# A hybrid decoder layer on one core: tile starts in SBUF moved to one distance modulo 512 bytes, low parts multiplied after high parts

## The chip, the cores and the metric

The kernel runs on one core of a Trainium2 chip. The time is device microseconds of one execution. The kernel before was timed in three runs, and a fourth execution was profiled; from that one come the rows shown below. The changed kernel is timed in the same way.

The engines are named as in the profile: PE is TensorE's matmul, PEld its load of the stationary operand (the weights of one matmul, 128 columns), DVE is VectorE, ACT ScalarE, POOL GpSimd, and SP issues DMAs.

## The reference: what is computed

One decoder layer on 512 positions of width 2048, in float32, cut to what matters here:

```python
h = rms_norm(x, norm1_w)
q, k, v, z, xbc, dt_raw = jnp.split(h @ w_in, SPLIT_POINTS, axis=-1)
attn = moba_attention(...)      # 8 heads of 128
ssm = ...                       # 16 heads of 64: conv(4), chunked scan, gate, grouped norm
x = x + jnp.concatenate([attn, ssm], axis=-1) @ w_out
h = rms_norm(x, norm2_w)
u = causal_dwconv(h @ w_up, ffn_conv_w, ffn_conv_b)
u_gate, u_val = jnp.split(u, 2, axis=-1)
return x + (jax.nn.silu(u_gate) * u_val) @ w_down
```

The four large products, with `w_in`, `w_out`, `w_up` and `w_down`, are nearly all of the work.

## The kernel before, in words

**Float32 by three products.** A float32 operand is held as a high part (rounded to the format that TensorE reads in one pass, written by ACT) and a low part (the operand minus its high part, written by DVE). A product of two operands is high by high, high by low, and low by high: three matmuls into the same PSUM accumulator. The activations' high and low parts are the tiles `A[k]` and `B[k]` (16 each, 128 x 512); those of a weight piece are the tiles `hi` and `lo`.

**The first stage** (`w_in`, attention, scan, `w_out`) takes its weights through a list of pieces. A chunk of 128 x 1024 is fetched into `raw`, and `issue_split` cuts it in two pieces, each with its own `hi` and `lo` tile from rings of three. The code keeps three pieces ahead: piece i + 3 is split after piece i has been multiplied. Three functions multiply a piece:

- `fm_uses`: features by positions. One accumulator of 512 columns; a piece holds four blocks of 128 x 128. Stationary is `hi` or `lo`, moving is `A` or `B`, 512 columns. A weight column block has four such pieces.
- `wide_use`: the same roles, but a piece is one k with four accumulators.
- `tok_use`: positions by features. Stationary is `A` or `B`, moving is `hi` or `lo`, with 256, 264 or 512 columns, four accumulators.

Between pieces the side work (norms, attention, scan) issues its own short matmuls into the `sm` tiles. The order of all engines is fixed when the program is built; a model of costs in the code (`Paced`) sets where side work is put in.

**The second stage** (`w_up`, `w_down`) multiplies 2 x 2 blocks with seven products in place of eight. A group has seven products, in the order P5, P3 of the group before, P1, P4 of the group before, P6, P2, P7. There are 44 groups for `w_up` (eight blocks of k, so 24 matmuls a product) and 24 for `w_down` (eight or seven blocks, so 24 or 21 matmuls). Stationary is a weight part (`hi2`, `lo2`, two or three buffers of 4096 bytes a partition), moving is one of seven combined activation tiles `cmb0` to `cmb6`, 256 columns. In each product the high parts come first (two matmuls for each block, lines 1288 and 1289) and the low parts last (line 1291). P3 reads `cmb5` (the name `K22` in the code), P4 reads `cmb6`; the other five products read `cmb0` to `cmb4`.

**Where tiles begin.** All numbers here are byte addresses in a partition as the program's allocation gives them, taken modulo 512. "Distance" below is the start of a matmul's moving operand minus the start of its stationary operand, modulo 512. Blocks of 128 columns are 512 bytes, so within a piece the distance stays the same, but for the second half of a piece with 264 columns, which is 32 bytes on.

| matmuls | distance before |
|---|---|
| first stage, `hi` with `A` or `B`, 512 columns moving | 256, 320, 384, by the buffer of the ring |
| first stage, `lo` with `A`, 512 columns moving | 64, 128, 192 |
| first stage, `hi` or `lo` moving | 128 to 480, by the buffer |
| second stage, six products of a group | 448 |
| second stage, P3 (`cmb5`) | 0 |

In the first stage the rings are 528 columns wide (2112 bytes, 64 more than a multiple of 512), so each buffer begins elsewhere. In the second stage a tile `space` of 112 columns (448 bytes) is allocated just before `cmb6`, so `cmb5` begins where the weight tiles begin and `cmb6` 448 bytes on.

## Time and profile before

| | us |
|---|---|
| median of three runs (2103.24 to 2107.04) | 2103.71 |
| profiled execution, its own time | 2103.83 |
| its span from the first to the last instruction | 2102.1 |

The page gives busy time by engine, then the chain of work that ended last, then groups of instructions. Two things are needed to read the rows of PE. A MATMUL's duration in the trace holds its latency, and matmuls overlap: a row's mean of 400 ns does not mean one matmul each 400 ns. What a matmul costs is the distance from its start to the next start, which the timeline shows, and which a window's length over its count of matmuls gives. And a window counts each instruction that reaches into it, so its count is up to two too high.

The stages stand at these times of the span: first stage up to 789 us, the change-over to about 831, `w_up` up to 1640, `w_down` up to the end.

### The profile page before, as it was taken

The page shows a single profiled execution, that of the slowest core. Times are in us where ns is not written, and L with a number is a line of the kernel's source. Part 1 is how long each engine was busy: PE and PEld are TensorE (multiplying, and loading weights), DVE is VectorE, ACT ScalarE, POOL GpSimd, SP SyncE. Part 2 cuts the span into 40 slices and gives each one's busy share as a digit, 9 for nine tenths or more (in the row PEclk, how much of TensorE's full clock was granted, in tenths as well). Part 3 has the DMA queues.
Part 4 walks back from the last instruction along what each step waited for, and adds up shares of the span by engine and source line. Part 5 has one row for each costly group of instructions (what it writes and reads, how often), then busy time and mean ns, then how long its engine had stood idle before and what let it go on. Part 6 is the DMA issues. An engine that isn't in the chain of part 4 may idle for free.

```text
span 2102.1 us, 37694 instructions
## 1 busy us (share of the span) xinstructions
PE 2061.9 (98%) x15366; PEld 1938.7 (92%) x15366; DVE 1582.6 (75%) x2251; ACT 988.3 (47%) x1433; POOL 207.9 (10%) x107
## 2 busy tenths in 40 slices
PE   9999999999999998999999999999999899999999
PEld 7888887888888888999999999999999799899999
DVE  6545555345565548999999999999999977977976
ACT  5433435244444435555555554555555534534532
POOL 0020000000000001101110111111111111101110
PEclk9999999999999999999999999999999999999999
DMA  5232222332224445445444444444355667856753
GB/s 196 73 116 91 71 72 79 92 109 81 79 72 162 158 134 193 158 152 191 151 154 178 167 162 159 165 181 161 141 191 202 216 214 245 272 188 232 261 202 121
DMA packets 114397, 328.19 MB, mean 156 GB/s; under 512 B 10736, under 2 KB 35120, under 8 KB 111408
## 3 DMA queue, kind: packets, MB, share of 16 engines
q1 hardware_dynamic: 114224, 325.78, 45.0%
q8 instruction: 121, 1.98, 0.4%
q14 instruction: 52, 0.43, 0.1%
HBM read 283.77 MB, written 41.98 MB: 155 GB/s over the span
## 4 chain that ended last, share of the span: by engine, by line
PE 90%; DVE 6%; DMA 2%; issue 1%; ACT 1%; SPq 0%; DVEq 0%; POOL 0%; ACTq 0%; POOLq 0%
PE acc L183 30%; PE x L1288 16%; PE x L1289 16%; PE x L1291 16%; PE sm L183 4%; PE y L1288 3%; PE y L1289 3%; PE y L1291 3%; DVE lo L1050 1%; DVE cmb L1097 1%; DMA rawa<-wd 1%; DMA ld<-gd 0%; DVE lo L183 0%; DVE acc L1153 0%; DVE s L1024 0%
## 5 line engine op out<-in xcount | busy, mean ns | idle before, releaser
L1289 PE MATMUL x<-cmb,hi 128*128 128x256 f32 x3168 | 748.5, 278 | 13.2 <-DVE cmb L1097 11.5
L1288 PE MATMUL x<-cmb,hi 128*128 128x256 f32 x3168 | 749.1, 278 | 11.9 <-ACT cP L1168 5.4
L1289 PEld LDWEIGHTS x<-cmb,hi 128*128 128x128 f32 x3168 | 597.4, 189 | 16.1 <-DVE cmb L1097 14.3
L1288 PEld LDWEIGHTS x<-cmb,hi 128*128 128x128 f32 x3168 | 596.9, 188 | 14.4 <-issue 7.9
L1291 PE MATMUL x<-cmb,lo 128*128 128x256 f32 x3168 | 430.3, 278 | 2.2 <-DVE lo L1050 2.0
L1291 PEld LDWEIGHTS x<-cmb,lo 128*128 128x128 f32 x3168 | 393.4, 189 | 2.7 <-DVE lo L1050 2.7
L183 DVE TENSOR_TENSOR lo<-raw,hi 128x512 fp32r<-128x512 f32 (+1 forms) x240 | 164.4, 691 | 242.3 <-ACT hi L183 227.7
L1041 ACT ACTIVATE hi<-s 128x1024 fp32r<-128x1024 f32 (+1 forms) x201 | 200.8, 999 | 284.8 <-DVE s L1024 190.4
L1017 POOL TENSOR_TENSOR rawb<-rawa,rawb 128x1024 f32<-128x1024 f32 (+1 forms) x68 | 169.6, 2495 | 1298.3 <-DVE s L1024 1061.8
L183 PE MATMUL acc<-A,hi 128*128 128x512 f32 x704 | 281.5, 400 | 0.7 <-ACT hi L183 0.7
L183 PE MATMUL acc<-A,lo 128*128 128x512 f32 x704 | 277.9, 395 | 0.1
L183 PE MATMUL acc<-B,hi 128*128 128x512 f32 x704 | 276.9, 393 | 0.0
L183 ACT ACTIVATE hi<-raw 128x512 fp32r<-128x512 f32 (+1 forms) x240 | 149.6, 629 | 255.7 <-PE acc L183 222.5
L1050 DVE TENSOR_TENSOR lo<-s,hi 128x1024 fp32r<-128x1024 f32 (+1 forms) x201 | 238.4, 1186 | 18.8 <-issue 18.8
L1050 DVE TENSOR_TENSOR lo<-rawa,hi 128x1024 fp32r<-128x1024 f32 (+1 forms) x204 | 241.5, 1184 | 3.9 <-PE x L1291 3.9
L1041 ACT ACTIVATE hi<-rawa 128x1024 fp32r<-128x1024 f32 (+1 forms) x204 | 209.6, 1028 | 40.2 <-PE x L1289 40.0
L183 PEld LDWEIGHTS acc<-A,lo 128*128 128x128 f32 x704 | 132.2, 188 | 32.3 <-DVE lo L183 1.4
L183 PEld LDWEIGHTS acc<-A,hi 128*128 128x128 f32 x704 | 132.8, 189 | 29.0 <-ACT hi L183 1.3
L183 PEld LDWEIGHTS acc<-B,hi 128*128 128x128 f32 x704 | 132.5, 188 | 28.3
L1168 ACT ACTIVATE cP<-x 128x256 f32<-128x256 f32 x132 | 50.8, 384 | 211.2 <-PE x L1291 211.2
L183 PE MATMUL acc<-hi,A 128*128 128x256 f32 (+2 forms) x448 | 135.5, 302 | 0.7 <-DVE u L183 0.7
L183 PE MATMUL acc<-lo,A 128*128 128x256 f32 (+2 forms) x448 | 133.7, 298 | 0.0
(204 smaller groups left out, 2775.1 us busy)
## 6 DMA issues: line engine op xcount, KB each, us to landing
rawa<-wu SPq DMA_DIRECT2D x176, 512.0 KB, 3.3
raw<-wi SPq DMA_DIRECT2D x79, 512.0 KB, 3.6
rawa<-wd SPq DMA_DIRECT2D x64, 448.0 KB, 4.2
rawb<-wu SPq DMA_DIRECT2D x44, 512.0 KB, 4.3
gd<-gt SPq DMA_DIRECT2D x22, 1024.0 KB, 4.4
raw<-wo SPq DMA_DIRECT2D x32, 512.0 KB, 3.5
rawa<-wd SPq DMA_DIRECT2D x32, 512.0 KB, 4.4
ld<-gd SPq DMA_DIRECT2D x27, 512.0 KB, 6.3
```

Of the source, the lines that this page charges most:

```text
L183: return fn(out, *args, **kw)
L1017: po.tensor_tensor(r, raw[gi, "11"][:, :n], r, op=OP.subtract)
L1041: se.activation(h[:, :n], src[:, :n], AF.Copy)
L1050: ve.tensor_tensor(l[:, :n], src[:, :n], h[:, :n].bitcast(F32), op=OP.subtract)
L1097: ve.tensor_tensor(lo, ld[:, :m, :], hi.bitcast(F32), op=OP.subtract)
L1168: se.activation(g[x], X[:, 256:] if x == "P5" else X[:, :256], AF.Copy)
L1288: pe.matmul(out, w, bk[:, 0, q, :], start=fresh and q == 0, stop=False, skip_group_check=True)
L1289: pe.matmul(out, w, bk[:, 1, q, :], start=False, stop=False, skip_group_check=True)
L1291: pe.matmul(out, l[:, q * 128:(q + 1) * 128], bk[:, 0, q, :], start=False, stop=q == n - 1, skip_group_check=True)
```

## The change

**Distances.** The rings `hi` and `lo` become 640 columns wide (2560 bytes, a multiple of 512), a tile `space` of 448 bytes is put before `A`, and pieces for `tok_use` begin 96 columns (384 bytes) into their tiles. The `space` of the second stage is allocated before `cmb5` in place of before `cmb6`. With that, by the allocation, every large product of both stages is at distance 448 (the second half of a 264-column piece at 480), but for some low parts.

**Low parts at distance 0.** Some pieces' low parts begin 112 columns (448 bytes) into their tile, which puts them at distance 0: the last of the four pieces of a column block in `fm_uses`; k = 3, 7, 11 in `wide_use`; the pieces with k0 = 4 and 8 in `tok_use`; and P3 of every fourth group of `w_up` and of every group of `w_down`. These are 176 matmuls with 512 columns, 64 with 256 and 32 with 264 in the first stage, and 264 in the second.

**Order.** In all pieces of `fm_uses`, and in those pieces of `wide_use` and `tok_use` whose low parts are at distance 0, all products with high parts are issued first and those with low parts last. No matmul, no transfer and no operation of ACT, DVE or POOL is added or taken away.

| matmuls | distance after |
|---|---|
| `A` with `hi`, `B` with `hi`, 512 columns | 448 (1408) |
| `A` with `lo`, 512 columns | 448 (536), 0 (168) |
| `hi` or `lo` moving, 512 columns | 448 (184), 0 (8) |
| moving, 256 columns, first stage | 448 (704), 0 (64) |
| moving, 264 columns | 448 and 480 (352), 0 and 32 (32) |
| second stage | 448 (10824), 0 (264) |

On PE, one piece of `fm_uses` in the first stage, before (`A_81` to `A_84` and `B_97` to `B_100` are the parts of four activation tiles):

```order
L183 MATMUL acc<-A_81,hi 128x512
L183 MATMUL acc<-B_97,hi 128x512
L183 MATMUL acc<-A_81,lo 128x512 [waits DVE_49]
L183 MATMUL acc<-A_82,hi 128x512
L183 MATMUL acc<-B_98,hi 128x512
L183 MATMUL acc<-A_82,lo 128x512
L183 MATMUL acc<-A_83,hi 128x512
```

The same piece now (the tiles' numbers are one higher):

```order
L183 MATMUL acc<-A_82,hi 128x512
L183 MATMUL acc<-B_98,hi 128x512
L183 MATMUL acc<-A_83,hi 128x512
L183 MATMUL acc<-B_99,hi 128x512
L183 MATMUL acc<-A_84,hi 128x512
L183 MATMUL acc<-B_100,hi 128x512
L183 MATMUL acc<-A_85,hi 128x512
L183 MATMUL acc<-B_101,hi 128x512
L183 MATMUL acc<-A_82,lo 128x512 [waits DVE_49]
L183 MATMUL acc<-A_83,lo 128x512
L183 MATMUL acc<-A_84,lo 128x512
L183 MATMUL acc<-A_85,lo 128x512
```

The four low parts, and the wait for DVE that stands before the first of them, have moved from between the high parts to the end of the piece.

DVE keeps its order, and so do ACT, POOL and SP; some of DVE's waits are others. At the change-over, before (`acc_s` is the first sum of the second stage):

```order
L183 TENSOR_TENSOR lo<-raw,hi 128x512 [waits PE_49,Activation_49]
L183 TENSOR_TENSOR rbc<-rbc,sq 128x512 [waits DVE_49,Activation_49]
L1024 TENSOR_TENSOR acc_s<-rawb,rawa 128x1024 [waits DMAHW4_49,DMAHW3_49]
L1050 TENSOR_TENSOR lo_7088<-acc_s,hi_7086 128x1024 [waits PE_49,Activation_49]
L183 TENSOR_TENSOR xin<-acc,xin 128x512 [waits DMAHW0_49,PE_49]
```

And now:

```order
L183 TENSOR_TENSOR lo<-raw,hi 128x512 [waits PE_49,Activation_49]
L183 TENSOR_TENSOR rbc<-rbc,sq 128x512 [waits DVE_49,Activation_49]
L1055 TENSOR_TENSOR acc_s<-rawb,rawa 128x1024 [waits DMAHW3_49,DMAHW4_49,DVE_49,PE_49]
L1083 TENSOR_TENSOR lo_7089<-acc_s,hi_7087 128x1024 [waits Activation_49]
L183 TENSOR_TENSOR xin<-acc,xin 128x512 [waits DMAHW0_49,PE_49]
```

`acc_s` now lies over one of the `lo` tiles of the last but one piece, and waits until PE has read it.

The diff:

```diff
@@ -210,6 +210,10 @@
 
 
     RW = 1024
+    WT, SHIFT_T, SHIFT_0 = 640, 96, 112
     BEHIND = 2.5
     pieces = []
 
@@ -245,12 +249,13 @@
             i = state["split"]
             ci, o, w, _ = pieces[i]
             issue_dma(ci)
-            h = wpool.tile([128, 528], F32R, name="hi")
-            l = wpool.tile([128, 528], F32R, name="lo")
+            ho, lo = getattr(pieces[i][3], "at", (0, 0))
+            h = wpool.tile([128, WT], F32R, name="hi")[:, ho:ho + w]
+            l = wpool.tile([128, WT], F32R, name="lo")[:, lo:lo + w]
             src = raws[ci][:, o:o + w]
             clk["last"] = ("pe", clk["pe"])
-            A_.activation(h[:, :w], src, AF.Copy)
-            V.tensor_tensor(l[:, :w], src, h[:, :w].bitcast(F32), op=OP.subtract)
+            A_.activation(h, src, AF.Copy)
+            V.tensor_tensor(l, src, h.bitcast(F32), op=OP.subtract)
             his[i] = (h, l)
             ready[i] = clk["dve"]
             state["split"] += 1
@@ -260,6 +265,7 @@
             nc.sync.dma_start(dbg[n], ap)
 
 
+    abp.tile([128, 112], F32, name="space")
     A = [abp.tile([128, S], F32R, name=f"A{k}") for k in range(NK)]
     B = [abp.tile([128, S], F32R, name=f"B{k}") for k in range(NK)]
     C = [cpool.tile([128, S], F32, name=f"C{k}") for k in range(NK)]
@@ -643,13 +649,19 @@
             def use(h, l, k0=k0, nk=nk):
                 if k0 == 0:
                     box["acc"] = acc_tile()
+                a = box["acc"]
+                w = lambda x, kk: x[:, kk * 128:(kk + 1) * 128]
                 for kk in range(nk):
                     k = k0 + kk
                     rh, rl = R(k)
-                    mm3(box["acc"], h[:, kk * 128:(kk + 1) * 128], l[:, kk * 128:(kk + 1) * 128], rh, rl,
-                        k == 0, k == nk_tot - 1)
+                    T.matmul(a, w(h, kk), rh, start=k == 0, stop=False)
+                    T.matmul(a, w(h, kk), rl, start=False, stop=False)
+                for kk in range(nk):
+                    T.matmul(a, w(l, kk), R(k0 + kk)[0], start=False, stop=k0 + kk == nk_tot - 1)
                 if k0 + nk == nk_tot:
-                    done(box["acc"])
+                    done(a)
+            if k0 + nk == nk_tot:
+                use.at = (0, SHIFT_0)
             uses.append(use)
             k0 += nk
         return uses
@@ -662,11 +674,21 @@
             if k == 0:
                 box["acc"] = [acc_tile() for _ in range(4)]
             rh, rl = R(k)
+            if k % 4 == 3 and k < NK - 1:
+                for t in range(4):
+                    ts_ = slice(t * 128, (t + 1) * 128)
+                    T.matmul(box["acc"][t], h[:, ts_], rh, start=False, stop=False)
+                    T.matmul(box["acc"][t], h[:, ts_], rl, start=False, stop=False)
+                for t in range(4):
+                    T.matmul(box["acc"][t], l[:, t * 128:(t + 1) * 128], rh, start=False, stop=False)
+                return
             for t in range(4):
                 ts_ = slice(t * 128, (t + 1) * 128)
                 mm3(box["acc"][t], h[:, ts_], l[:, ts_], rh, rl, k == 0, k == NK - 1)
                 if k == NK - 1:
                     done(t, box["acc"][t])
+        if k % 4 == 3 and k < NK - 1:
+            use.at = (0, SHIFT_0)
         return use
 
     def tok_use(k0, nk, cols, box, done):
@@ -675,6 +697,13 @@
             if k0 == 0:
                 box["acc"] = [acc_tile() for _ in range(4)]
             edge = k0 == 0 or k0 + nk == NK
+            if again:
+                for part, x in ((h, A), (h, B), (l, A)):
+                    for kk in range(nk):
+                        for t in range(4):
+                            T.matmul(box["acc"][t][:, :cols], x[k0 + kk][:, t * 128:(t + 1) * 128],
+                                     part[:, kk * cols:(kk + 1) * cols], start=False, stop=False)
+                return
             order = [(kk, t) for t in range(4) for kk in range(nk)] if edge else \
                     [(kk, t) for kk in range(nk) for t in range(4)]
             for kk, t in order:
@@ -687,6 +716,8 @@
                 T.matmul(o, B[k][:, ts_], h[:, cc], start=False, stop=k == NK - 1)
                 if k == NK - 1:
                     done(t, box["acc"][t])
+        again = k0 in (4, 8)
+        use.at = (SHIFT_T, SHIFT_0 if again else SHIFT_T)
         return use
 
     XR = lambda k: (A[k], B[k])
@@ -1046,7 +1077,9 @@
             return
         n = cols(items[k][0])
         h, src = parts[k]
-        l = lp.tile([128, 1024], F32R, name="lo2", bufs=2)
+        l = lp.tile([128, 1152], F32R, name="lo2", bufs=2)
+        if items[k][1] == "P3" and (items[k][0] % 4 == 0 or items[k][0] >= NF and items[k][0] % 1 == 0):
+            l = l[:, SHIFT_0:]
         ve.tensor_tensor(l[:, :n], src[:, :n], h[:, :n].bitcast(F32), op=OP.subtract)
         parts[k] = (h, l)
 
@@ -1125,7 +1158,7 @@
 
     def x_split(n):
         t, h = (K22, KT4)[n // 2], n % 2
-        if n == 2:
+        if n == 0:
             lp.tile([128, 112], F32, name="space")
         if h == 0:
             up_kinds[t] = cmb_tile(t)
```

## The prediction

> **What bounds the kernel now.** I read the page's first lines and its chain, then busy time by stage, then PE alone in order of time. The first two rows are the page's, the other four those of a view by windows (window, length, busy us of each engine, granted clock, share and rate of DMA):
>
> ```profile
> PE 2061.9 (98%) x15366; PEld 1938.7 (92%) x15366; DVE 1582.6 (75%) x2251; ACT 988.3 (47%) x1433; POOL 207.9 (10%) x107
> PE 90%; DVE 6%; DMA 2%; issue 1%; ACT 1%; SPq 0%; DVEq 0%; POOL 0%; ACTq 0%; POOLq 0%
> ...
> 0.00:789.30 789.30, 781.78 (x4266) 664.86 (x4266) 414.32 (x794) 340.27 (x639) 36.32 (x38) 1.00 0.33 106
> 789.30:831.00 41.70, 33.62 (x269) 33.05 (x270) 32.47 (x41) 20.16 (x29) 6.68 (x3) 0.92 0.57 202
> 831.00:1640.00 809.00, 809.00 (x7082) 809.00 (x7081) 761.05 (x947) 426.62 (x550) 104.09 (x43) 1.00 0.46 166
> 1640.00:2102.00 462.00, 437.53 (x3755) 431.75 (x3753) 374.79 (x472) 201.24 (x216) 60.77 (x24) 1.00 0.64 221
> ```
>
> PE bounds every stage but the 40 us of change-over: it idles 7.5 us in the first stage, nothing in `w_up`, 24.5 us in `w_down`. No other engine is near it in the first stage (DVE 414 of 789 us); in `w_up` DVE has 48 us to spare in 809. So what a matmul costs, start to start, is the question. PE in order of time, three products of one `w_up` group (P3, P1, P4; start, duration, with the first high part of each, the row of its eight low parts, and the start of the next product):
>
> ```profile
> 834.58 0.28 PE L1288 MATMUL x<-cmb,hi 128*128 128x256 f32 x1
> ...
> 837.30 0.28 PE L1288 MATMUL x<-cmb,hi 128*128 128x256 f32 x1
> ...
> 839.20 1.12 PE L1291 MATMUL x<-cmb,lo 128*128 128x256 f32 x8
> 840.16 0.29 PE L1288 MATMUL x<-cmb,hi 128*128 128x256 f32 x1
> ...
> 842.90 0.28 PE L1288 MATMUL x<-cmb,hi 128*128 128x256 f32 x1
> ...
> 844.72 1.07 PE L1291 MATMUL x<-cmb,lo 128*128 128x256 f32 x8
> 845.62 0.28 PE L1288 MATMUL x<-cmb,hi 128*128 128x256 f32 x1
> ```
>
> P5 (834.58 to 837.30) and P4 (842.90 to 845.62) take 2.72 us for 24 matmuls, 113.3 ns each. P3, the one product at distance 0, takes 2.86 us: 118.8 ns for a high part, 120.0 for a low part, and the product behind it 2.74. Same shapes, same engine, nothing waited for: what differs is where `cmb5` begins. I read this as the weight load and the moving stream meeting in SBUF.
>
> Distance 448 alone does not give 113.3, though. At the change-over, `cmb` products at distance 448, then the first P3 of the program (818.08):
>
> ```profile
> 811.99 0.28 PE L1288 MATMUL x<-cmb,hi 128*128 128x256 f32 x1
> ...
> 813.87 1.10 PE L1291 MATMUL x<-cmb,lo 128*128 128x256 f32 x8
> ...
> 818.08 0.28 PE L1288 MATMUL x<-cmb,hi 128*128 128x256 f32 x1
> ...
> 819.99 1.12 PE L1291 MATMUL x<-cmb,lo 128*128 128x256 f32 x8
> ...
> 822.79 1.08 PE L1291 MATMUL x<-cmb,lo 128*128 128x256 f32 x8
> ...
> 825.51 1.07 PE L1291 MATMUL x<-cmb,lo 128*128 128x256 f32 x8
> ```
>
> Sixteen high parts in 813.87 − 811.99 = 1.88 us are 117.5 ns each: a slower rhythm that began behind a stall and held, at 448, until P3's run at distance 0; from the low parts of the product behind P3 to those of the next, 822.79 to 825.51, it is 113.3 again (2.72 / 24). So 448 has two rhythms, and a run at distance 0 ends the slow one. That is what I take the low parts at distance 0 to do in the changed kernel.
>
> The first stage has neither. Windows over accumulator matmuls alone (264, 512, 256 columns moving, then 512 columns of `A` and `B`), and the counts:
>
> ```profile
> 95.98:125.28 29.30, 29.30 (x241) 1.00 0.38 109
> 381.40:425.60 44.20, 44.20 (x193) 1.00 0.29 92
> 473.60:490.60 17.00, 16.99 (x144) 1.00 0.22 64
> 640.00:770.00 130.00, 128.73 (x556) 1.00 0.51 166
> ...
> L183 PE MATMUL acc<-A,hi 128*128 128x512 f32 x704 | 281.5, 400 | 0.7 <-ACT hi L183 0.7
> L183 PE MATMUL acc<-hi,A 128*128 128x256 f32 x256 | 73.5, 287 | 0.0
> L183 PE MATMUL acc<-hi,A 128*128 128x264 f32 x128 | 36.8, 288 | 0.7 <-DVE u L183 0.7
> L183 PE MATMUL acc<-lo,A 128*128 128x512 f32 x64 | 25.2, 394 | 0.0
> ```
>
> With 512 columns a matmul costs 231.5 ns (128.73 / 556; 230 where `A` is stationary, 44.20 / 192), with 256 columns 118.1 (17.00 / 144), with 264 columns 122.1 (29.30 / 240); the pieces stand at all three distances of the rings. Each row of counts stands three times (high-high, high-low, low-high): 3 × (704 + 64) = 2304 with 512 columns, 768 with 256, 384 with 264. The first is 533 us, two thirds of the stage.
>
> **The change part by part.** The sum is made against the profiled execution's 2103.83 us; the median of the runs is 0.12 lower.
>
> *P3.* In 33 groups of `w_up` all of P3 goes to 448: 2.86 + 2.74 becomes 2 × 2.72, 0.16 us each, 5.3. In 11 groups and the 24 of `w_down` only its high parts do: 16 × (118.8 − 113.3) = 0.09 us, 35 × 0.09 = 3.1. Together 8.4. If it were hidden by DVE it would be nothing; DVE's 761 of 809 us leaves 1.1 us a group, seven times the gain. `w_down` has waits in which part of its 2.1 may vanish.
>
> *The 512-column matmuls.* No row shows one in a stream at 448, so its cost is bounded. From above: 231.5, no gain. From below, the half clock at the change-over, where 256 columns take as long as 512 at full clock (ten starts on):
>
> ```profile
> 801.05 0.41 PE L1289 MATMUL x<-cmb,hi 128*128 128x256 f32 x1
> ...
> 803.18 0.42 PE L1289 MATMUL x<-cmb,hi 128*128 128x256 f32 x1
> ```
>
> 2.13 us / 10 = 213 ns, so 256 columns at full clock are 106.5 and the fast rhythm adds 6.8 to that. The same 6.8 on 213 gives 220; the slow rhythm (11 more than 106.5) 224. Pieces here are cut by side work and stalls, after which either rhythm may come, and the runs at distance 0 stand some 11 us apart (48 × 231 ns); two thirds fast, a third slow gives 221.5, and I take 222. That is 9.5 ns on the 2304 − 176 = 2128 matmuls at 448: 20.2 us. The ends are 0 and 18.5 × 2128 = 39 us.
>
> The Trainium skill ("TensorE: Matmul & The Clock Gate", Back-to-back issue gap) states N / 2.4 + 2.5 ns, 215.8 for 512 columns; by that the term would be an estimated 33 us. For 256 columns it gives 109.2, which no stretch of this trace reaches (113.3).
>
> *256 and 264 columns.* 118.1 to about 114.5 on 704, 2.5 us; 122.1 to 118 on 352, 1.4 us (ends 0 and 3.4 + 1.9).
>
> *Order and waits.* The same matmuls and loads run in another order. PE waited for DVE's low parts before and does so eight matmuls later now, which can only shorten a wait; such waits are 7.5 us of the stage at most. DVE's new waits stand where a `lo` ring buffer is read last in its piece; the next write is three pieces ahead, and behind it stand only side vector operations. I cost them at nothing; uncovered, the low parts of a piece (8 × 0.12 us) on 14 pieces would be 13 us of DVE, which is idle for 375 us there. At the change-over `acc_s` waits for the last but one piece:
>
> ```profile
> 785.32 0.40 PE L183 MATMUL acc<-A,lo 128*128 128x512 f32 x1
> 785.56 0.40 PE L183 MATMUL acc<-A,hi 128*128 128x512 f32 x1
> ...
> 785.95 1.22 DVE L1024 TENSOR_TENSOR acc_s<-rawb,rawa 128x1024 f32<-128x1024 f32 x1 [3.44 <-DMA rawa<-wu]
> ```
>
> That piece ends at 785.56, `acc_s` starts at 785.95 on a DMA: 0.4 us of cover. Without it the whole change-over shifts by as much. Transfers follow the same rings, so they start earlier with PE, at a third of the DMA engines' time.
>
> Sum: 8.4 + 20.2 + 2.5 + 1.4 = 32.5 us. 2103.83 − 32.5 = 2071.3, less 0.12: **2071**.
>
> **The rivals.**
>
> *Only the 256-column matmuls feel the distance.* With 512 columns the load takes half of the stream, and may find its way anywhere. For it: no row shows it otherwise; against it: 231.5 is 18 above 213, more than the 256's 11.6, so something costs there, and a matmul in three at 448 among others at other distances could not settle. 2103.7 − 8.4 − 2.5 − 1.4 = 2091.
>
> *The loss at 512 vanishes whole.* 214 to 217 ns: 14.5 to 17.5 × 2128 = 31 to 37 us, with the other terms 2055 to 2061. For it: the weight load has half the stream free. Against it: no stretch at full clock shows less than 6.8 of overhead.
>
> *The slow rhythm holds.* The place is P3 of the first group: before, 24 matmuls at distance 0 ended the slow rhythm, now 8 have to. If 8 are too few, `w_up` runs at 117.5: a group costs 7 × 2.82 = 19.74 us against 6 × 2.72 + 2.88 = 19.20, 44 × 0.54 = 24 us more, and `w_down` up to 13 more. The first stage, with the same short runs, then stays at 224 at best and 231.5 at worst: 2103.7 + 24 − 16 = 2112 to 2127, say 2118. It decides when a run leaves the next product above 117. Against it: in P3 at 837.30 the high parts are at 118.8 on average, near its low parts' 120, so the state turns early.
>
> *The distance is not the cause.* P3 might be slow for its place in the group. The Trainium skill ("SBUF — State Buffer", Who interferes with whom) says that PE never waits on anyone, and that its two read ports are independent; by that rule a distance would cost nothing; the trace differs, with 2.86 against 2.72 us. Were P3's place the cause, the change would move nothing: 2103.7. For its place speaks nothing in the rows: it reads and writes as P6 does.
>
> **How the numbers follow.** My forecast (222 ± 3 ns with 512 columns: 2064 to 2079) 0.57; only 256-column matmuls 0.20; the loss vanishes whole 0.12; slow rhythm 0.06; distance not the cause 0.05. The range takes in the forecast, the first two rivals and their bounds: 2055 to 2094; the forecast's own is 2064 to 2079. A measurement of this kernel tells 0.2% (4 us) from no change. Faster: 0.57 + 0.20 + 0.12 = 0.89; within 0.2%, where the distance is not the cause: 0.05; slower, the slow rhythm: 0.06.
>
> **What would show it.** Right: windows over 512-column pieces in 640 to 750 at 219 to 225 ns a matmul; P3 as long as P4 in three of four `w_up` groups; a product behind a run of low parts at 113 to 114 after a stall; the first stage some 24 us shorter, the change-over as long. Wrong: 231 ns in the first stage; 117.5 ns over many groups of `w_up`; new waits for DVE in PE's rows, above all in `w_up`, where DVE's share rises to 95%.

## The result, and the profile after

The changed kernel takes 2136.08 us (median of four executions, 2134.34 to 2138.36) where the kernel before takes 2104.42 (2103.24 to 2107.04): a ratio of 1.0149, 95% interval 1.0132 to 1.0167. It is slower by some 32 us. I had said 2071, faster, with 0.06 for slower.

First the page of the changed kernel (busy time by engine; chain by engine), then its stages by windows (window, length, busy us and count of PE, PEld, DVE, ACT, POOL, granted clock, share and rate of DMA). The ends of the windows are put where the stages end now.

```profile
PE 2100.5 (98%) x15366; PEld 1974.2 (92%) x15366; DVE 1587.3 (74%) x2251; ACT 988.2 (46%) x1433; POOL 208.4 (10%) x107
PE 90%; DVE 7%; issue 2%; ACT 1%; DMA 1%; SPq 0%; DVEq 0%; POOL 0%; ACTq 0%; POOLq 0%
...
0.00:792.00 792.00, 785.53 (x4266) 664.95 (x4266) 415.52 (x795) 339.86 (x639) 36.69 (x38) 1.00 0.33 105
792.00:833.50 41.50, 32.70 (x262) 31.92 (x263) 32.47 (x39) 20.07 (x29) 6.75 (x3) 0.92 0.58 203
833.50:1666.70 833.20, 833.20 (x7098) 833.20 (x7097) 764.94 (x950) 428.18 (x551) 105.64 (x43) 1.00 0.44 162
1666.70:2136.00 469.30, 449.05 (x3745) 444.15 (x3744) 374.37 (x470) 200.10 (x214) 59.32 (x24) 0.99 0.63 216
```

The instruction counts, the chain and DVE's time are those of before. `w_up` takes 833.2 us where it took 809.0 (the window now holds 16 matmuls more, some 2 us; `w_down` lacks ten); `w_down` 469.3 for 462.0; the first stage 792.0 for 789.3; the change-over 41.5 for 41.7. From the first matmul of group 2 to that of group 44, the same work in both, it is 828.8 us (837.88 to 1666.63) for 806.4 (834.58 to 1640.98), and from there to the end 466.9 for 458.1. In `w_up` PE never idles in either kernel, so each matmul costs more there: 117.4 ns (833.20 / 7098) for 114.2.

Where it turns can be seen on one page of PE in order of time (start, duration; the first high part of a product, or its row of eight low parts). These are P5 and then P3 of group 4, the second P3 with low parts at distance 0, then P1, P4 and P6:

```profile
895.00 0.28 PE L1321 MATMUL x<-cmb,hi 128*128 128x256 f32 x1
...
897.72 0.28 PE L1321 MATMUL x<-cmb,hi 128*128 128x256 f32 x1
...
899.53 1.12 PE L1324 MATMUL x<-cmb,lo 128*128 128x256 f32 x8
900.49 0.28 PE L1321 MATMUL x<-cmb,hi 128*128 128x256 f32 x1
...
903.32 0.28 PE L1321 MATMUL x<-cmb,hi 128*128 128x256 f32 x1
...
906.14 0.28 PE L1321 MATMUL x<-cmb,hi 128*128 128x256 f32 x1
```

P5 takes 2.72 us, and the sixteen high parts of P3, now at 448, 1.81 (113.1 ns each): the fast rhythm, with P3 in it, as predicted. The eight low parts at distance 0 take 0.96 (120 ns). Behind them P1 takes 2.83 and P4 2.82 us, 117.7 ns a matmul, and so it stays to the end of `w_up`, over nine more runs at distance 0. What I had put there to end the slow rhythm starts it, and doesn't end it.

The first stage, windows over accumulator matmuls alone (512, 256, 264 columns):

```profile
640.00:770.00 130.00, 128.10 (x550) 1.00 0.50 164
475.70:492.40 16.70, 16.66 (x144) 1.00 0.21 65
96.50:125.60 29.10, 29.09 (x241) 1.00 0.36 104
```

With 512 columns a matmul costs 128.10 / 550 = 232.9 ns, more than the 231.5 of before (from start to start in that window 233.1 for 232.3, as the counts take in two matmuls too many); with 256 columns 116.0 (118.1 before), with 264 columns 121.3 (122.1).

### The profile page after: what moved, and what is told of

It reads as the page before. It is cut to its first block, busy times and chain, and to the rows that moved or that the text cites. A ratio compares the mean times of both kernels' runs of the same rounds, so it can differ in the third digit from the quotient of the medians.

```text
span 2136.7 us, 37701 instructions
## 1 busy us (share of the span) xinstructions
PE 2100.5 (98%) x15366; PEld 1974.2 (92%) x15366; DVE 1587.3 (74%) x2251; ACT 988.2 (46%) x1433; POOL 208.4 (10%) x107
## 4 chain that ended last, share of the span: by engine, by line
PE 90%; DVE 7%; issue 2%; ACT 1%; DMA 1%; SPq 0%; DVEq 0%; POOL 0%; ACTq 0%; POOLq 0%
PE acc L183 30%; PE x L1324 16%; PE x L1322 16%; PE x L1321 16%; PE sm L183 4%; PE y L1322 3%; PE y L1324 3%; PE y L1321 3%; DVE lo L1083 2%; DVE cmb L1130 1%; DVE acc L1186 0%; DVE s L1055 0%; DVE lo L183 0%; DVE s L1061 0%; DMA t<-xT 0%
## 5 line engine op out<-in xcount | busy, mean ns | idle before, releaser
L1321 PE MATMUL x<-cmb,hi 128*128 128x256 f32 x3168 | 766.4, 281 | 11.8 <-ACT cP L1201 7.5
L1322 PE MATMUL x<-cmb,hi 128*128 128x256 f32 x3168 | 766.0, 281 | 10.0 <-DVE cmb L1130 10.0
L1324 PE MATMUL x<-cmb,lo 128*128 128x256 f32 x3168 | 440.0, 281 | 2.6 <-DVE lo L1083 2.6
L1324 PEld LDWEIGHTS x<-cmb,lo 128*128 128x128 f32 x3168 | 401.4, 189 | 3.2 <-DVE lo L1083 3.2
L183 PE MATMUL acc<-A,lo 128*128 128x512 f32 x704 | 205.1, 395 | 0.0
L1322 PE MATMUL y<-cmb,hi 128*128 128x256 f32 x528 | 128.0, 282 | 3.1 <-DVE cmb L1130 3.1
L1321 PE MATMUL y<-cmb,hi 128*128 128x256 f32 x528 | 127.6, 281 | 0.0
```

The source lines that it names most:

```text
L183: return fn(out, *args, **kw)
L1321: pe.matmul(out, w, bk[:, 0, q, :], start=fresh and q == 0, stop=False, skip_group_check=True)
L1322: pe.matmul(out, w, bk[:, 1, q, :], start=False, stop=False, skip_group_check=True)
L1324: pe.matmul(out, l[:, q * 128:(q + 1) * 128], bk[:, 0, q, :], start=False, stop=q == n - 1, skip_group_check=True)
```

## The experiments

In all of them "at 448" and so on is the distance as defined above, "rhythm" is the start-to-start time of 256-column matmuls, 113.3 ns or 117.8 ns, and a shift of 16 columns is 64 bytes. A P3 is named by its own group; it runs behind P5 of the next. Numbers in ns without a row are the same kind of difference between starts as those with one.

### Which stage loses

Second stage of the changed kernel behind the first stage of the kernel before (the diff is against the kernel before):

```diff
+        l = lp.tile([128, 1152], F32R, name="lo2", bufs=2)
+        if items[k][1] == "P3" and (items[k][0] % 4 == 0 or items[k][0] >= NF and items[k][0] % 1 == 0):
+            l = l[:, 112:]
-        if n == 2:
+        if n == 0:
             lp.tile([128, 112], F32, name="space")
```

> The kernel before with the second stage of the changed one alone (space ahead of cmb5, eight low parts at distance 0); the first stage keeps its rings of 528 columns and its order. If the second stage holds the whole loss: 2131 to 2136 us, the first stage as before. If the first stage lost the time: about 2104 us.

And the first stage of the changed kernel with the second stage of the kernel before (against the changed kernel):

```diff
-        l = lp.tile([128, 1152], F32R, name="lo2", bufs=2)
-        if items[k][1] == "P3" and (items[k][0] % 4 == 0 or items[k][0] >= NF and items[k][0] % 1 == 0):
-            l = l[:, SHIFT_0:]
+        l = lp.tile([128, 1024], F32R, name="lo2", bufs=2)
-        if n == 0:
+        if n == 2:
             lp.tile([128, 112], F32, name="space")
```

> The changed kernel with the second stage of the one before (cmb5 and so all of P3 at distance 0, cmb6 at 448). If the first stage neither gained nor lost (512 columns at 448 cost 233.2 ns against 231.5, 256 columns 116.5 against 118): 2103 to 2108 us, the second stage at 113.4 ns outside P3. If the first stage's order or distances hold the loss: about 2134 us.

The second stage alone: 2138.09 us, ratio 1.0156 (1.0139 to 1.0173). The first alone: 2104.98, ratio 0.9998 (0.9989 to 1.0008). One window of `w_up` of each (second stage alone, then first stage alone):

```profile
830.00:1640.00 810.00, 810.00 (x6878) 810.00 (x6878) 741.36 (x921) 413.55 (x533) 100.77 (x41) 1.00 0.44 162
```

```profile
830.00:1640.00 810.00, 810.00 (x7090) 810.00 (x7089) 761.86 (x947) 426.52 (x550) 103.87 (x43) 1.00 0.46 166
```

810 us hold 6878 matmuls (117.8 ns) in the one and 7090 (114.2) in the other. So the whole loss is the second stage's, and the first stage is worth nothing either way (the 2.7 us by which it was longer in the changed kernel's profiled execution don't come back in these ten). In the second stage alone `w_up` came out of the change-over in the slow rhythm, and none of eleven runs at distance 0 ended it.

### The runs at distance 0 taken out

The changed kernel without its shifted low parts in the second stage:

```diff
         l = lp.tile([128, 1152], F32R, name="lo2", bufs=2)
-        if items[k][1] == "P3" and (items[k][0] % 4 == 0 or items[k][0] >= NF and items[k][0] % 1 == 0):
-            l = l[:, SHIFT_0:]
```

> The changed kernel, but in the second stage no low part is put at distance 0: all of it stands at 448. Theory A (a run of eight low parts at distance 0 throws PE from the 113.4 ns rhythm into the 117.8 ns one, and at 448 either rhythm lasts until something disturbs it): w_up stays at 113.4 ns once it is there, some 30 us less in w_up and up to 12 less in w_down, 2094 to 2106 us. Theory B (at 448 PE falls into the slow rhythm by itself and only whole P3 products at 0, 24 matmuls each group, pull it out): 117.8 ns throughout, 2132 to 2142 us.

Its ten executions fall in two groups, so a ratio means nothing: 2094.82 to 2098.53 (four) and 2125.87 to 2130.29 (six), with 2105.08 for the kernel before beside them. The profiled one is of the second group:

```profile
830.00:1640.00 810.00, 810.00 (x6880) 810.00 (x6879) 741.28 (x920) 413.95 (x534) 100.78 (x41) 1.00 0.44 161
```

117.7 ns in all of `w_up`, at 448 throughout. In `w_down` of the same execution, behind waits, there are long stretches at 113.3 with the same starts. So both rhythms keep themselves going at 448, and which one comes behind a stall is not fixed by the starts. That the quick group had `w_up` at 113.3 was not seen in a trace, but the gap fits: 43 groups by 168 matmuls by 4.5 ns are 32.5 us, and the groups lie 27 to 35 us apart.

### Is it the length of the run?

Changed kernel; in `w_up` P3 of some groups has whole, low or high parts shifted by a table (`hi2` is 1152 columns wide, too; nothing is shifted in `w_down`):

```diff
+    W, L, H = (112, 112), (0, 112), (112, 0)
+    RUNS = {1: W, 3: W, 5: L, 7: L, 9: H, 11: H, 13: W, ..., 20: (0, 16), 23: (0, 32), 26: (0, 64), 29: (0, 96), ...}
-        h = lp.tile([128, 1024], F32R, name="hi2", bufs=3)
+        h = lp.tile([128, 1152], F32R, name="hi2", bufs=3)
+        h = h[:, RUNS.get(gi, (0, 0))[0] if x == "P3" else 0:]
```

> The changed kernel with another table of runs at distance 0 in P3 of w_up: by group the whole product (16 high and 8 low parts), its 8 low parts alone, its 16 high parts alone, or none, and in four groups the low parts at 384, 320, 192 or 64; none in w_down. Theory A: behind 8 low parts at 0 the rhythm is 117.8 ns whichever it was ahead, behind a whole product 113.4 ns whichever it was ahead, and groups with none keep the rhythm that they come in with. Theory B: whole products lead to 113.4 ns, groups with none fall back to 117.8. The 16 high parts alone and the low parts at other distances are open: no number is expected.

2126.85 us (one execution). PE in order of time: P3 of group 1, whole at distance 0, then P1 and the start of P4:

```profile
838.72 0.28 PE L1324 MATMUL x<-cmb,hi 128*128 128x256 f32 x1
...
841.60 0.28 PE L1324 MATMUL x<-cmb,hi 128*128 128x256 f32 x1
...
844.42 0.28 PE L1324 MATMUL x<-cmb,hi 128*128 128x256 f32 x1
```

P3 takes 2.88 us (120.0 ns), and P1 behind it 2.82 (117.5). All 24 matmuls at distance 0, as many as in the kernel before, and the slow rhythm holds; so it did behind every run of the table (all were entered slow, so what they leave behind the fast rhythm this execution doesn't show). That the run was merely too short fell with this. The eight low parts alone at 384, 320, 192 or 64 (groups 20, 23, 26, 29) left it slow as well. What is left as a difference: in the kernel before, the moving tile `cmb5` begins elsewhere and the weights stay; here the weights begin elsewhere and `cmb5` stays.

### Runs made by the moving tile

Kernel before, with `cmb5` where it was (32 bytes past a multiple of 512, the other `cmb` 480), and P3's weights shifted by a table:

```diff
+    Z, F = (0, 0), (16, 16)
+    RUNS = {0: Z, 3: (16, 0), 4: (16, 0), 5: Z, 6: (0, 16), 7: (0, 16), 8: Z, 9: (16, 0), 10: Z, 11: Z, 12: (32, 32), ...}
+    run_of = lambda gi: RUNS.get(gi, F)
+        h = h[:, run_of(gi)[0] if x == "P3" else 0:]
+        l = l[:, run_of(items[k][0])[1] if items[k][1] == "P3" else 0:]
```

> The kernel before with one change: in P3 the weight parts begin some columns into their tiles, by a table (hi2 and lo2 are 1152 columns wide). cmb5 stays where it was, 32 bytes past a multiple of 512, so P3 is at distance 0 without a shift, at 448 with a shift of 16 columns, at 384, 320, ... with 32, 48, ... . In the run with the table of shifted weights the runs at distance 0 were made by moving the weights, and none of them, not even a whole P3, ended the slow rhythm; in the kernel before the weights stay and the moving tile begins elsewhere. Theory C (what ends the slow rhythm is a whole run at distance 0 that is entered and left by the moving operand's start): groups 0, 5, 8, 11, 13, ... (whole P3 at 0) leave 113.3 ns behind them, whatever was ahead; groups with 16 columns (448) change nothing; low parts alone at 0 (groups 3, 4, 9) or high parts alone (6, 7) may leave either, and I expect 117.8 behind low parts alone, as in the changed kernel; from group 24 on, all at 448, the rhythm stays what group 23 left, 113.3. Time near 2095 to 2103. Rival (the exit is chance, and the kernel before was lucky in its alignment): whole runs at 0 leave 117.8 in some groups and 113.3 in others; time 2100 to 2126.

2102.5 us (one execution). P3 of group 3 (high parts at 448, the eight low parts alone at 0), with P1 and the start of P4; then P3 of group 15 (whole at 0), which comes out of the slow rhythm:

```profile
875.08 0.28 PE L1296 MATMUL x<-cmb,hi 128*128 128x256 f32 x1
...
876.97 1.12 PE L1299 MATMUL x<-cmb,lo 128*128 128x256 f32 x8
877.93 0.29 PE L1296 MATMUL x<-cmb,hi 128*128 128x256 f32 x1
...
880.66 0.28 PE L1296 MATMUL x<-cmb,hi 128*128 128x256 f32 x1
...
1105.86 0.28 PE L1296 MATMUL x<-cmb,hi 128*128 128x256 f32 x1
...
1108.73 0.29 PE L1296 MATMUL x<-cmb,hi 128*128 128x256 f32 x1
...
1111.47 0.28 PE L1296 MATMUL x<-cmb,hi 128*128 128x256 f32 x1
```

Eight low parts at distance 0 are followed by 2.73 us (877.93 to 880.66), the fast rhythm; against my expectation for low parts alone. The whole run, entered at 117.8, is followed by 2.74. So 24 matmuls at distance 0 end the slow rhythm here and did not in the table before: at the same length, the place of the tiles decides. Eight of them keep the fast rhythm here, where in the changed kernel eight ended it; whether eight would also end the slow one here was not run. In what it says of whole runs at 0 theory C held: behind none of them was the rhythm left slow, and the rival fell. One thing came out that no theory had: the high parts of group 3, at 448, cost 118.1 (1.89 / 16) between products at 113.5 and 114.1. With both tiles 64 bytes on, the same distance is in the other rhythm, and going back restores the first.

| P3's distance (`cmb5` at 32) | P3, ns, entered at 113.3 | P1 behind it |
|---|---|---|
| 0 and 256 | 119.2 | 114.1 (fast) |
| 128 and 384 | 118.3, 118.4 | 114.1 (fast) |
| 192 and 448 | 117.6 | 114.2 (fast) |
| 64 and 320 | 113.4 | 117.9 (slow) |

Distances 256 bytes apart behave alike.

### Whole runs kept, but rare

The kernel before with the same two lines and another rule in place of the table, P3 at 448 by a shift of 16 columns but for every eighth group of `w_up` and every second of `w_down`:

```diff
+    run_of = lambda gi: (0, 0) if gi % (8 if gi < NF else 2) == 0 else (16, 16)
```

> The kernel before, with P3 at distance 448 by weights that begin 16 columns into their tiles, except in every eighth group of w_up and every second of w_down, where P3 stays whole at distance 0 as before. First stage as before. Theory C: the first P3 ends the slow rhythm as in the kernel before, every eighth would again, and the other P3 take 2.72 us in place of 2.86, the product behind them 2.72 for 2.74: 38 groups of w_up by 0.16 and 12 of w_down by 0.16 are 8.0 us, so 2105 - 8 = 2097, in every execution. Rival (rhythm by chance): some executions near 2097, others near 2126, as in the run with no runs at distance 0.

2102.71 us (2101.80 to 2104.80), ratio 0.999 (0.998 to 0.9999). All ten executions are near there, so the fast rhythm holds in each, but the gain is 2.5 us and not 8. P3 of group 11, then P1 and the start of P4:

```profile
1029.62 0.28 PE L1292 MATMUL x<-cmb,hi 128*128 128x256 f32 x1
...
1032.44 0.29 PE L1292 MATMUL x<-cmb,hi 128*128 128x256 f32 x1
...
1035.18 0.28 PE L1292 MATMUL x<-cmb,hi 128*128 128x256 f32 x1
```

P3 takes 2.82 us and P1 2.74, not 2.72 each: 448 with both tiles 64 bytes on is not 448.

### What a 512-column matmul costs at each distance

Changed kernel; each column block of `fm_uses` has its parts 16 columns further than the block before, modulo eight (`sweep` counts the pieces, four to a block); the blocks of `tok_use` with 256 and 264 columns are moved in the same way:

```diff
-            if k0 + nk == nk_tot:
-                use.at = (0, SHIFT_0)
+            use.at = (sweep(),) * 2
```

> The changed kernel with other starts in its first stage: each column block of fm_uses has its high and low parts 16 columns further than the block before it, modulo eight, so blocks stand at distances 448, 384, 320, ... 0; blocks of tok_use with 256 and 264 columns move likewise. What each theory expects of 512 columns: if the distance sets the cost of a 512-column matmul at all, some distance shows clearly under 231 ns in its undisturbed stretches (my prediction's 222 would be one of them), and I would have chosen the wrong one; if 512 columns don't feel it, all eight distances stand within 2 ns of each other at 231 to 233. I expect the second: the kernel before had 230 to 231.7 at nine starts, the changed one 231.2 at 0 and 233.3 at 448. The second stage is that of the changed kernel, so the time is near 2136 in both cases.

In `w_out` such blocks follow each other without a break. These are the starts of nine blocks of 48 matmuls, at distances 384, 320, 256, 192, 128, 64, 0, 448 and 384:

```profile
664.91 0.39 PE L183 MATMUL acc<-A,hi 128*128 128x512 f32 x1
...
676.07 0.40 PE L183 MATMUL acc<-A,hi 128*128 128x512 f32 x1
...
687.07 0.40 PE L183 MATMUL acc<-A,hi 128*128 128x512 f32 x1
...
697.97 0.40 PE L183 MATMUL acc<-A,hi 128*128 128x512 f32 x1
...
709.17 0.39 PE L183 MATMUL acc<-A,hi 128*128 128x512 f32 x1
...
720.33 0.40 PE L183 MATMUL acc<-A,hi 128*128 128x512 f32 x1
...
731.32 0.40 PE L183 MATMUL acc<-A,hi 128*128 128x512 f32 x1
...
742.22 0.40 PE L183 MATMUL acc<-A,hi 128*128 128x512 f32 x1
...
753.42 0.39 PE L183 MATMUL acc<-A,hi 128*128 128x512 f32 x1
```

| distance | us for 48 | ns each |
|---|---|---|
| 0, 256 | 10.90, 10.90 | 227.1 |
| 64, 320 | 10.99, 11.00 | 229.0 |
| 128, 384 | 11.16, 11.16 | 232.5 |
| 192, 448 | 11.20, 11.20 | 233.3 |

This expectation was wrong, on the side of the other theory: 512 columns do feel the distance, modulo 256, and 448 is the dearest of the eight. My forecast went to the right variable and to the wrong end of it. The kernel as a whole took 2135.64 us (one execution); its second stage is that of the changed kernel.

The table is one for blocks that stand at one distance, and here only the weights were moved. The kernel before mixes distances within a piece. By the table its pieces of `w_out` should cost, on the mean of a piece, 227.7 ns (high parts at 256, low parts at 64), 230.2 (320 and 128) and 232.8 (384 and 192); between 655 and 778 us of its trace they cost 232.6, 232.9 and 231.7, with a low part behind every two high parts. With the same starts and the low parts last, as in the trace of the next section, it is 229.9, 231.1 and 232.8. So the table holds the better the longer the distance stays, and the neighbours of a matmul count too.

### The order alone

The kernel before with the changed kernel's order in `fm_uses`, `wide_use` and `tok_use`, every tile where it was:

```diff
-                    mm3(box["acc"], h[...], l[...], rh, rl, k == 0, k == nk_tot - 1)
+                    T.matmul(a, w(h, kk), rh, start=k == 0, stop=False)
+                    T.matmul(a, w(h, kk), rl, start=False, stop=False)
+                for kk in range(nk):
+                    T.matmul(a, w(l, kk), R(k0 + kk)[0], start=False, stop=k0 + kk == nk_tot - 1)
```

> The kernel before with the changed kernel's order of products in the first stage (high parts of a piece first, low parts last) and nothing moved: all tiles begin where they did. My prediction cost the order at nothing. Expected: within 2 us of the kernel before, 2103 to 2107. Rival: the order has a price or gain of its own (its stalls, or 512-column matmuls that cost more or less because the distance changes less often), and the changed kernel's first stage, which came out even, hides it: more than 3 us either way.

2102.94 us, ratio 0.9991 (0.9981 to 1.0000): a gain of some 2 us, by the interval between none and 4.

### The first stage at its good distance

Changed kernel with all 512-column matmuls at distance 256 (the line `use.at = (48, 48)` in `fm_uses` and in `wide_use`, the last line in `tok_use`), and the second stage of the kernel with rare whole runs:

```diff
-            if k0 + nk == nk_tot:
-                use.at = (0, SHIFT_0)
+            use.at = (48, 48)
-        use.at = (SHIFT_T, SHIFT_0 if again else SHIFT_T)
+        use.at = (48, 48) if cols == 512 else (SHIFT_T, SHIFT_T)
```

> First stage of the changed kernel with all 512-column matmuls at distance 256 in place of 448 and 0 (256 and 264 columns stay at 448 and 480), second stage of the kernel with rare whole runs. If the distance modulo 256 sets the cost of 512 columns, each of the 2304 costs 228 ns in place of the 231.7 of the kernel before: 8.5 us less than the kernel with rare whole runs, near 2102.7 - 8.5 - 2 (256 columns) = 2092. Rival (the 228 of the sweep came from changing blocks or from chance): the first stage is as long as before, and the time near 2101 to 2103.

2091.73 us (2088.72 to 2093.77), ratio 0.9941 (0.9925 to 0.9958), 2092 expected. The window over 512-column matmuls:

```profile
640.00:770.00 130.00, 130.00 (x575) 1.00 0.51 166
```

130.00 / 575 = 226.1 ns, 5.4 less than before in the same window (from start to start 226.7 for 232.3).

### What ends the slow rhythm, and what starts it

The changed kernel with `cmb5` at 480 as the others. In `w_up` P3 of odd groups is shifted whole by 112 columns, P3 of even groups by 8, 16, ... 104; then high or low parts alone. `w_down` and the first stage have sweeps in steps of 4 columns:

```diff
+    RUNS = {g: (112, 112) for g in range(1, 44, 2)}
+    RUNS.update({2 * i + 2: (8 * i + 8, 8 * i + 8) for i in range(13)})
+    RUNS.update({28: (0, 16), 30: (16, 0), 32: (0, 48), 34: (48, 0), 36: (0, 80), 38: (80, 0), ...})
```

> The changed kernel with three tables. First stage: column blocks of fm_uses at starts in steps of 4 columns (16 bytes), sixteen of them, so distances 448, 432, ... 208. w_up: all at 448 with cmb5 480 bytes past a multiple of 512, P3 alone shifted by its weights: in odd groups whole P3 by 112 columns (distance 0), in even groups by 8, 16, ... 104 columns, then high or low parts alone. w_down: all products of seven in a row share one shift, 4 to 96 columns. From the two earlier sweeps: 512 columns repeat with 256 bytes (228 ns at 0 and 256, 229.4 at 64 and 320, 232.5 at 128 and 384, 233.2 at 192 and 448). Theory D (there are two phases of weight load against moving stream; the place of both tiles modulo 256 sets what each phase costs, and which phase a run leaves): odd groups leave 117.8, as in the run with the table of shifted weights; some shift of the even groups, perhaps 16 columns (weights at 96 modulo 256, as in P3 of the run by the moving tile) or 80, leaves 113.3 from the slow phase; the first stage's costs lie on a smooth curve through the four known ones with its least near 0 modulo 256, 227 to 228. Rival (the phase can be changed to the fast one only by a run whose moving tile begins elsewhere): no even group leaves 113.3. Time 2120 to 2140.

2135.43 us (one execution). P5, P3 of group 8 (32 columns, distance 320), P1, P4; then, behind P6, P2 and P7, P5, P3 of group 9 (112 columns, distance 0), P1, P4:

```profile
974.09 0.28 PE L1338 MATMUL x<-cmb,hi 128*128 128x256 f32 x1
...
976.93 0.28 PE L1338 MATMUL x<-cmb,hi 128*128 128x256 f32 x1
...
979.75 0.28 PE L1338 MATMUL x<-cmb,hi 128*128 128x256 f32 x1
...
982.47 0.28 PE L1338 MATMUL x<-cmb,hi 128*128 128x256 f32 x1
...
993.35 0.28 PE L1338 MATMUL x<-cmb,hi 128*128 128x256 f32 x1
...
996.07 0.28 PE L1338 MATMUL x<-cmb,hi 128*128 128x256 f32 x1
...
998.95 0.28 PE L1338 MATMUL x<-cmb,hi 128*128 128x256 f32 x1
...
1001.77 0.28 PE L1338 MATMUL x<-cmb,hi 128*128 128x256 f32 x1
```

P5 comes in at 2.84 us, P3 at distance 320 takes 2.82, and P1 behind it 2.72: the slow rhythm ended with no run at 0. P5 comes in at 2.72, P3 at 0 takes 2.88, and P1 behind it 2.82: started again. After distance 0 made by the weights the rhythm was slow in every odd group up to 41, whether it was entered fast or slow (behind 43 a wait comes between). Of the other shifts, entered slow, those to 416, 352, 320, 288, 160, 96, 64 and 32 left 113.3 to 114.0; those to 384, 256, 224, 192 and 128 left 117.8. High parts alone at 384 or 128 left 113.3, low parts alone there 117.8. So a run can change the rhythm with the moving tile in its place; the rival fell. It is not the distance of a run alone that decides: whole products at 320 and 64 ended the slow rhythm, and low parts alone at 320 and 64, in the run with the first table, did not.

In the first stage of this run the finer steps gave no smooth curve. In the unbroken blocks of `w_out`: 226.7 ns at 272, 227.0 at 256, 233.3 at 288, 233.4 at 240, 229.1 at 320. That part of the expectation was wrong. (With the blocks that waits interrupt, 256 comes to 228.6, which made 272 look better than it is.)

Then those that had ended it, each twice, entered from the fast rhythm; first stage at 256 as above:

```diff
+    RUNS = {0: (40, 40)}
+    for i, r in enumerate(((8, 8), (24, 24), (32, 32), (40, 40), (72, 72), (88, 88), (96, 96), (104, 104), (16, 0), (80, 0))):
+        RUNS[4 * i + 2] = RUNS[4 * i + 4] = r
+    run_of = lambda gi: RUNS.get(gi, (0, 0)) if gi < NF else (40, 40) if gi % 2 == 0 else (0, 0)
```

> First stage with 512 columns at distance 256, second stage all at 448 with cmb5 as in the changed kernel, and P3 shifted by its weights in group 0 (40 columns, distance 288), in pairs of groups of w_up (2 and 4: 8 columns; 6 and 8: 24; 10 and 12: 32; 14 and 16: 40; 18 and 20: 72; 22 and 24: 88; 26 and 28: 96; 30 and 32: 104; 34 and 36: high parts alone by 16; 38 and 40: high parts alone by 80), and by 40 in every second group of w_down. Each of these ten left 113.3 ns when it came out of the slow rhythm in the run with finer distances. Theory D (the place of both tiles modulo 256 sets which phase a run leaves, whatever was ahead): each leaves 113.3 when it comes out of the fast rhythm too, so from group 1 on every product that isn't shifted is at 113.3 to 114; the shifted P3 cost 117 to 120. Rival (such a run turns the phase round, slow to fast and fast to slow): the first of each pair leaves 117.8, the second 113.3. Time by D: 2091.7 less some 5 for P3 at 113.3 in most groups, 2087; by the rival half of w_up at 117.8, 2100.

2084.99 us (one execution). All twenty leave the fast rhythm (113.3 to 113.6), so they don't turn it round: at these starts the fast rhythm is left whatever was ahead. Most cost something themselves (116.5 to 120.1 ns), but two don't. P5, P3 of group 10 at distance 320, P1 and the start of P4:

```profile
994.82 0.28 PE L1324 MATMUL x<-cmb,hi 128*128 128x256 f32 x1
...
997.54 0.28 PE L1324 MATMUL x<-cmb,hi 128*128 128x256 f32 x1
...
1000.26 0.28 PE L1324 MATMUL x<-cmb,hi 128*128 128x256 f32 x1
...
1002.98 0.28 PE L1324 MATMUL x<-cmb,hi 128*128 128x256 f32 x1
```

2.72 us three times: 320 (and 64) costs nothing in the fast rhythm and ends the slow one.

### Both put together

The changed kernel with other starts only: P3 of every group at 320, P6 in `w_down` too, and the first stage at 272 (44 columns in `fm_uses` and `wide_use`; `A` and `B` stationary stay at 256).

```diff
+    run_of = lambda gi, x: 32 if x == "P3" or x == "P6" and gi >= NF else 0
+        h = h[:, run_of(gi, x):]
+        l = l[:, run_of(*items[k]):]
-                use.at = (0, SHIFT_0)
+            use.at = (44, 44)
```

> The changed kernel with other starts only: 512-column matmuls of the first stage at distance 272 (192 of them, with A and B stationary, at 256), P3 of every group, and P6 of the groups of w_down, shifted by 32 columns to distance 320, all else of the second stage at 448. In the run with pairs of shifted groups P3 at 320 cost 113.3 ns when it was entered in the fast rhythm, and 320 left the fast rhythm behind it whatever was ahead. Theory D: w_up at 113.3 from the second group on, in every execution; against that run (2085.0, one execution) 1.6 us less for its sixteen dearer P3 of w_up (mean 4.5 ns by 24 matmuls each), 1.1 us less in w_down, 1.4 us less at 272 (226.96 against 227.6 ns on 2112): 2081, between 2078 and 2084. Rival (320 isn't safe in every state; a stall brings a phase from which it leaves the slow rhythm): some executions 10 to 30 us longer.

2084.83 us (2084.67 to 2084.91), ratio 0.9902 (0.9885 to 0.9918): the fastest of all, 21 us under the kernel before, and its four executions lie within 0.24 us. `w_up`, and the 512-column window:

```profile
822.90:1624.00 801.10, 801.10 (x7071) 801.10 (x7071) 759.64 (x946) 426.81 (x550) 103.93 (x43) 1.00 0.46 168
...
640.00:770.00 130.00, 130.00 (x571) 1.00 0.50 165
```

801.10 / 7071 = 113.3 ns over all of `w_up`. Of the 2081 expected, `w_up` gave its part. The first stage gave nothing: 272 costs 227.7 ns (130.00 / 571; from start to start 228.3), more than the 226.1 (226.7) at 256, so the 226.7 of one block of the finer sweep doesn't carry over to a stage that stands at 272 throughout. `w_down` gave nothing either (459.0 us to the end of the span at about the same time as in the run before, 458.6), although nearly all its undisturbed products are at 113.3: its waits take up what its matmuls save.

## Why the prediction was wrong, step by step

**What bounds the kernel: right.** PE's start-to-start time set every stage but the change-over, before and after. In `w_down` PE's idle time fell from 24.5 to 20.3 us, so there its waits took up a part of the loss.

**"A run at distance 0 ends the slow one": the step that failed.** The rows behind it were read rightly (117.5 ahead of the first P3, 113.3 behind it), but all 68 P3 of the trace stand at one and the same pair of starts modulo 512, and I took distance for what they have in common. The runs showed: at distance 0 with weights and `cmb5` 480 past a multiple of 512 the rhythm is left slow, by 24 matmuls as by 8; with both 32 past it is left fast. The change makes its runs the first way. That cost some 22 us in `w_up` and 9 in `w_down`.

**The rival "the slow rhythm holds" is what happened**, with a chance of 0.06. Its prices were good: 24 for `w_up`, up to 13 for `w_down`, with some 22 and 9 measured. Its total of 2112 to 2127 was too low because it left `w_down`'s term out: 2127 and 9 are the 2136 measured. Its reason was not the one shown: 24 matmuls at the new starts didn't end the slow rhythm either, and in the profiled execution the runs started it in group 4 rather than fail to end it. My argument against it, that P3's high parts already stood at 118.8, was about P3 and not about what follows. Its chance should have been near that of a coin: the run at 0 was moved to other starts, and no row showed one there.

**512-column matmuls: 222 ns forecast, 233 measured.** The term of 20.2 us came out as a loss of about (232.9 − 231.5) × 2128 = 3 us, or 2 by the starts (233.1 for 232.3). The step that failed is the carrying over of 448 from 256 columns: 448 is where 256 columns have their fast rhythm, and where 512 columns are dearest. The bound from below (213 at the clock, plus 6.8) was reached nowhere; the best, from start to start, was 226.7.

**The rival "only 256-column matmuls feel the distance"** was wrong too: 227.1 to 233.3 by distance alone. **"The loss vanishes whole"** happened at none of the distances tried. That a load takes only half of the stream is not shown here: in the 512-column window of the kernel before, loads are recorded as busy for 104 of 130 us.

**256 and 264 columns.** 118.1 to 116.0 and 122.1 to 121.3, for 114.5 and 118: 1.5 and 0.3 us in place of 2.5 and 1.4. Some of these pieces run at 115, others at 119.6, at the same starts.

**P3: right in size where the rhythm is fast** (2.72 us at 448, groups 1 to 3), and the gain went with the rhythm.

**Order, waits, change-over at nothing: right.** Order alone 0.9991 (0.9981 to 1.0000); the change-over 41.5 us for 41.7. The small loss with 512 columns and the small gains of order and of 256 columns cancel; that the first stage is worth nothing (0.9998) is measured, this split of it is argued.

**The sum.** Of the 65 us between 2071 and 2136, some 31 are the slow rhythm of the second stage, 8 the gain of P3 that went with it, 22 the 512-column term and 2 the 256 and 264 columns; the other 2 are not accounted for. Small slips in the working decided nothing: two thirds of 220 and a third of 224 are 221.3, not 221.5, and 222 ± 3 gives 2065 to 2078.

**The range** held only fast rhythms in `w_up`. In the kernel with the runs taken out, ten executions fell four to six: a rhythm that a stall can flip needs both of its times in the range.

## What to carry to other kernels

Where a stage is a stream of weight loads and matmuls, sweep the start of one operand against the other before believing any one distance, per shape: here one kernel with a different start in each block gave the whole table. A pattern that occurs often but always at the same addresses is one observation, not many. And where the same addresses run at two speeds, look for a placement that always leads back to the faster one, and time several executions.

## What the runs showed that I had not expected

- With 512 columns moving, in blocks that stand at one distance, the distance between moving and stationary start sets the cost, modulo 256 bytes: 227.1, 229.0, 232.5, 233.3 ns at 0, 64, 128, 192. The Trainium skill ("TensorE: Matmul & The Clock Gate", Step-by-step: what each phase is for) says that loading the next tile's weights takes no read bandwidth from the running matmul. The trace doesn't fit a load that costs the matmul nothing, as nothing but starts was changed between those blocks; whether it is read bandwidth that is lost, no run here shows.
- With 256 columns in the second stage at 448 (and 192, 64, 320) there are two rhythms, 113.3 and 117.8 ns; at 448 both last for hundreds of products. At 0 and 128 modulo 256 there was only one cost, 118 to 120.
- Which rhythm is left behind by a whole product at another start goes by where both tiles begin, and not by their distance: 0 left the fast one with both at 32, the slow one with both at 480, wherever no wait came between. Parts of a product can do otherwise than the whole: at 384, entered slow, the whole and the low parts left the slow rhythm, the high parts alone the fast one.
- What stays open: why. No run looked below the level of starts and intervals, and why 320 leads back to the fast rhythm for nothing is not explained, only repeated: in the last kernel it did so wherever no wait came between.
